# Memory rows in the order of their loads, its late pieces on SyncE between the weight chunks, and a new order for x's norms

## The chip, the cores and the metric

The kernel runs on one core of a Trainium2 chip. The metric is device time in microseconds (us) of one execution, lower is better. Before the change three runs gave 817.77, 818.16 and 818.42 us (median 818.16).

## What is computed

One encoder layer on `x` (512 rows of 1024 columns, float32) with 256 memory rows `mem`. The start, which the change touches, is this part of the reference:

```python
u = rmsnorm(h, g_mix[l])
proj = u @ w_in[l]
...
mkv = rmsnorm(mem, g_mem[l]) @ w_mem_kv[l]
mk, mv = jnp.split(mkv, 2, axis=-1)
```

After it come three branches (gated linear attention, forgetting attention, attention into the memory rows), which are gated, merged, projected and added to `x`; then an MLP with squared ReLU and a last norm. None of that is touched.

## The kernel before, in words

Every float32 operand is split in two: `hi` is the value cast to fp32r (on ScalarE), `lo` is the rest (a subtraction on VectorE). A product is three matmuls: hi by hi, hi by lo, lo by hi. TensorE's order is written out by hand; the other engines' instructions are placed by a scheduler, with `issue_after` (here `behind`) fixing the order where it matters. Weights come as chunks of 128x1024 from `wst`, in the order of `chunk_list`.

The start, in the pool "front", runs like this:

- **Warm-up.** Ten matmuls of zeros (`wz`, L288) on TensorE, which nothing waits for.
- **Loads.** SyncE issues, in this order: `cols_s` (L289: 24 columns with `g_mix`, `g_mem` and `g_gla_head`), the memory-key weight chunks 0 to 3 (L268, `raw`; chunk 0 in two halves), chunk 4 (the first of the memory-value weights), two row tiles of `x` (L314, `xn`), the identity (L331, a part of `cst_s`), chunk 5, and two more tiles of `x`. ScalarE issues the transposed memory `memr` in four pieces of two k-tiles each (L291). A k-tile is 128 of the 1024 columns of `mem`.
- **Keys.** For each k-tile, ScalarE forms `mxh` = memory times `g_mem` (L299) and VectorE `mxl` (L301); for each half chunk ScalarE casts `hi` (L272) and VectorE forms `lo` (L274). TensorE needs both: 12 matmuls of 256 columns for each k-tile (`mem_keys`, L353), 8 k-tiles.
- **Values.** 12 matmuls of 512 columns for each of the value chunks 4 and 5 (`mem_values`, L367). Chunks 6 and 7 follow between the transposes, with weights that come through L140, L147 and L148 (`raw`, `whi`, `wlo`).
- **x.** For each row tile t: sum of squares on ScalarE (L320, `xsq`, `ssx`), `ms` on VectorE (L216), its power of -1/2 on GpSimd (L217, `rr`), and the scaling in place on VectorE (L323). Then TensorE transposes `xn` against the identity (L381): k-tiles 0 and 1 first, row tiles 0 to 2 of both and then row tile 3 of both. For each k-tile `uhi` (ScalarE, L384) and `ulo` (VectorE, L385) empty the PSUM bank, and the bank is then free for a later k-tile.

From there on TensorE works through the projections (L157 to L159) and the rest of the layer.

A tile of the pool "weights" has three buffers, so chunk 5 takes the buffer of chunk 0 when that one's `lo` is done, and the weights after it follow in the same way. A transfer also carries one of eight completion counters in turn (DMAHW0 to DMAHW7 in the rows below); the ninth waits until the first has landed, and so on.

Of the kernel before, what the change touches and what calls it, by code (L numbers as in the profile page):

```python
# [9 lines left out]
F32 = mybir.dt.float32  # L10
# [51 lines left out]


@with_exitstack
def hybrid_block(ctx, tc, chunks, wst, memT, xN, cols, gffn, gfin, wup, cst, out):
    nc = tc.nc
    PSUM = bass.MemoryType.PSUM
    index = {c: i for i, c in enumerate(chunks)}
# [3 lines left out]
    def nm(s):  # L72
        uid[0] += 1
        return f"{s}_{uid[0]}"
# [28 lines left out]
    gmix, gmem, ghead = cols_s[:, 0:8], cols_s[:, 8:16], cols_s[:, 16:20]  # L103
# [109 lines left out]
    def rsqrt(pool_, ss, inv, n):  # L213
        ms = pool_.tile([P, n], F32, tag="ms", name=nm("ms"), bufs=2)
        r = pool_.tile([P, n], F32, tag="rr", name=nm("rr"), bufs=2)
        nc.vector.tensor_scalar(ms, ss, inv, EPS, op0=ALU.mult, op1=ALU.add)  # L216
        nc.gpsimd.tensor_tensor(r, ms, mhalf[:, :n], op=ALU.pow)  # L217
        return r
# [33 lines left out]

    with pool("front") as fp:
        rmb = gv[:, 0, 0:M]
        memr = fp.tile([P, KT, M], F32, name="memr")
        xn = fp.tile([P, NT, D], F32, name="xn")
        ssx = small(fp, NT, "ssx")
        pre = {}

        def lead(key, loads=1, parts=1, after=(None, None, None)):  # L260

            late = index[key] in (3, 4)
            raw = (fp if late else wp).tile([P, 1024], F32, tag="lead" if late else "raw", name=nm("raw"), bufs=2 if late else 3)
            hi, lo = pre[key] = [wp.tile([P, 1024], F32R, tag=g, name=nm(g)) for g in ("hi", "lo")]
            for i in range(loads):
                sl = slice(i * 1024 // loads, (i + 1) * 1024 // loads)
                with behind(after[0]):
                    d = nc.sync.dma_start(raw[:, sl], wst[index[key]][:, sl]).ins  # L268
            for i in range(parts):
                sl = slice(i * 1024 // parts, (i + 1) * 1024 // parts)  # L270
                with behind(after[1]):
                    a = nc.scalar.copy(hi[:, sl], raw[:, sl]).ins  # L272
                with behind(after[2]):
                    v = nc.vector.tensor_tensor(lo[:, sl], raw[:, sl], f(hi[:, sl]), op=ALU.subtract).ins  # L274
# [9 lines left out]
        warm = fp.tile([P, 1], F32, name="warm")  # L284
        nc.vector.memset(warm, 0.0)
        ps = at_()
        for _ in range(10):
            nc.tensor.matmul(ps, wz[:, :P], wz, start=True, stop=True)  # L288
        nc.sync.dma_start(cols_s, cols)  # L289
# [4 lines left out]
        vec = None  # L294
        for j in range(4):
            parts = None
            for k in (2 * j, 2 * j + 1):
                with behind(act):
                    act = nc.scalar.mul(mxh[:, k, :], memr[:, k, :], gmem[:, k:k + 1]).ins  # L299
                with behind(vec):  # L300
                    vec = nc.vector.scalar_tensor_tensor(mxl[:, k, :], memr[:, k, :], gmem[:, k:k + 1], f(mxh[:, k, :]),  # L301
                                                         op0=ALU.mult, op1=ALU.subtract).ins
                if parts is None:
                    parts = lead(chunks[j], 1 if j else 2, 2, (None, act, vec))
                    _, act, vec = next(parts)
# [4 lines left out]
        load, act, vec = next(lead(chunks[4], after=(None, act, vec)))  # L310
# [5 lines left out]
        def x_norm(t):  # L316

            sq = fp.tile([P, D], F32, tag="xsq", name=nm("xsq"), bufs=2)
            with behind(act):
                a = nc.scalar.activation(sq, xn[:, t, :], AF.Square, accum_out=ssx[:, t:t + 1]).ins  # L320
            with behind(vec):
                r = rsqrt(fp, ssx[:, t:t + 1], 1.0 / D, 1)
            return a, nc.vector.tensor_scalar(xn[:, t, :], xn[:, t, :], r, None, op0=ALU.mult).ins  # L323
# [1161 lines left out]
def layout(inputs):  # L1485
# [3 lines left out]
    x = np.asarray(inputs["x"])[0]  # L1489
    mem = np.asarray(inputs["mem"])[0]  # L1490
    chunks = chunk_list()
    wst = np.zeros((len(chunks), P, 1024), np.float32)
    for i, c in enumerate(chunks):
# [4 lines left out]
        elif c[0] == "B":  # L1498
            _, q, h, (kh, ch) = c
            j = 8 * q + 4 * h + int(kh) - 1  # L1500
# [9 lines left out]
        elif c[0] == "F":  # L1510
            _, q, h, (kh, ch) = c
            ks = slice(512 * (int(kh) - 1), 512 * int(kh))
            for n in range(2):
                j = 8 * q + 4 * h + 2 * n + int(ch) - 1
                b = W["w_ff1"][ks, j * P:(j + 1) * P].reshape(4, P, P).transpose(1, 0, 2)
# [3 lines left out]
        else:  # L1519
            g = wst[i].reshape(P, KT, P)  # L1520
# [10 lines left out]
    cols[:, 16:20] = np.asarray(inputs["g_gla_head"])[0].T  # L1531
    wup = np.zeros((P, 264), np.float32)
    wup[0:16, 0:256] = np.asarray(inputs["w_alpha_up"])[0]
    wup[16:24, 256:264] = np.eye(8, dtype=np.float32)
# [12 lines left out]
    cst[:, 4 * P:5 * P] = same & (s > t)  # L1547
    cst[:, 5 * P:] = np.where(t > s, np.float32(NEG), 0.0)
    arrays = {
        "wst": wst, "memT": tl(mem), "xN": np.ascontiguousarray(x), "cols": cols,  # L1550
        "gffn": np.ascontiguousarray(np.broadcast_to(np.asarray(inputs["g_ffn"])[0], (P, D))),
        "gfin": np.ascontiguousarray(np.broadcast_to(np.asarray(inputs["g_final"]), (P, D))),
        "wup": wup, "cst": cst,
# [24 lines left out]
```

## Time and profile before

| | |
|---|---|
| median of 3 runs | 818.16 us (817.77 to 818.42) |
| the profiled execution | 817.71 us |
| its span, first to last instruction | 815.9 us |
| TensorE busy | 805.8 us (99% of the span) |
| VectorE, ScalarE, GpSimd busy | 590.5, 438.5, 103.3 us |
| first matmul on real data starts | 6.28 us |
| first transposes of x start | 24.69 us |

In rows of the timeline the columns are start, duration, engine, line, operation, output<-inputs, count, and in brackets the idle time before it with what ended it. A row in which several instructions are merged has the time of all of them. "SPq" and "ACTq" are the issue of transfers by SyncE and ScalarE, not the transfers. A matmul's duration includes its way through the array, so two in a row overlap: what one costs in a stream is the distance from start to start.

### The profile page before, as it was taken

To read this page: it belongs to the slowest core of one execution; us is meant where nothing else is said; L and a number is where in the kernel's file an instruction comes from. 1 tells how busy PE (TensorE), PEld (TensorE's weight loads), DVE (VectorE), ACT (ScalarE), POOL (GpSimd) and SP (SyncE) were. 2 spreads that over 40 slices of the span, in tenths; PEclk is the share of its full clock that TensorE was granted. 3 is DMA by queue.
4 is the path that set the end of the run, shared out by engine and by line. 5 is a ranking of instruction groups with operands and counts; after the bars stand their busy time and mean duration, and the time that the engine had idled before them with its cause. 6 is when DMAs were issued, how large, how long until landed. Compare 5 with 4: busy or idle time off the path is not lost.

```text
span 815.9 us, 12429 instructions
## 1 busy us (share of the span) xinstructions
PE 805.8 (99%) x4789; PEld 707.8 (87%) x4789; DVE 590.5 (72%) x912; ACT 438.5 (54%) x694; POOL 103.3 (13%) x126
## 2 busy tenths in 40 slices
PE   8999999999999999999999999999999999999996
PEld 6888888888888888999999889988998899889984
DVE  5756878636465577877567648896789778887896
ACT  7745655543345234444444526774676467647764
POOL 0000110010101112134133000011001100100011
PEclk9999999999999999999999999999999999999998
DMA  9534667589689876767755604878758966896643
GB/s 337 180 104 155 181 181 202 178 235 260 189 233 278 232 232 182 164 172 187 203 152 155 206 2 160 269 161 223 236 170 190 218 213 176 192 251 200 157 81 126
DMA packets 38748, 155.53 MB, mean 191 GB/s; under 512 B 4704, under 2 KB 5152, under 8 KB 36640
## 3 DMA queue, kind: packets, MB, share of 16 engines
q1 hardware_dynamic: 27280, 95.47, 33.6%
q0 software_dynamic: 9328, 54.01, 32.0%
q10 hardware_dynamic: 2080, 5.26, 2.0%
q8 instruction: 37, 0.61, 0.3%
q14 instruction: 23, 0.19, 0.1%
HBM read 152.58 MB, written 31.49 MB: 226 GB/s over the span
## 4 chain that ended last, share of the span: by engine, by line
PE 96%; DVE 1%; DMA 1%; issue 1%; ACT 0%; SPq 0%; POOL 0%; POOLq 0%; DVEq 0%; ACTq 0%
PE mm L157 24%; PE mm L159 24%; PE mm L158 24%; PE a L158 5%; PE a L157 5%; PE a L159 5%; PE a L367 1%; PE mm L353 1%; DMA raw<-in_wst_dram 1%; PE a L597 1%; PE a L635 1%; PE a L634 1%; DVE h L1240 1%; PE a L873 1%; DVE lo L1246 0%
## 5 line engine op out<-in xcount | busy, mean ns | idle before, releaser
L148 DVE TENSOR_TENSOR wlo<-raw,whi 128x1024 fp32r<-128x1024 f32 x67 | 86.6, 1297 | 58.9 <-ACT whi L147 58.5
L157 PE MATMUL mm<-uhi,whi 128*128 128x512 f32 (+1 forms) x352 | 125.9, 358 | 0.0
L159 PE MATMUL mm<-uhi,wlo 128*128 128x512 f32 (+1 forms) x352 | 123.7, 351 | 0.0
L158 PE MATMUL mm<-ulo,whi 128*128 128x512 f32 (+1 forms) x352 | 123.6, 351 | 0.0
L147 ACT CAST whi<-raw 128x1024 fp32r<-128x1024 f32 x67 | 70.5, 1052 | 91.5 <-PE mm L158 55.0
L1244 ACT CAST hi<-raw 128x1024 fp32r<-128x1024 f32 x65 | 68.2, 1049 | 49.6 <-PE mm L158 34.4
L1246 DVE TENSOR_TENSOR lo<-raw,hi 128x1024 fp32r<-128x1024 f32 x65 | 79.5, 1222 | 17.4 <-ACT hi L1244 17.4
L157 PEld LDWEIGHTS mm<-uhi,whi 128*128 128x128 f32 x352 | 66.7, 189 | 9.9 <-issue 1.4
L159 PEld LDWEIGHTS mm<-uhi,wlo 128*128 128x128 f32 x352 | 66.6, 189 | 9.1
L158 PEld LDWEIGHTS mm<-ulo,whi 128*128 128x128 f32 x352 | 66.7, 189 | 8.1
L1244 ACT CAST hi<-b 128x1024 fp32r<-128x1024 f32 x40 | 41.9, 1048 | 42.0 <-PE mm L159 25.5
L158 PE MATMUL mm<-u2l,hi 128*128 128x256 f32 x224 | 63.4, 283 | 0.0
L159 PE MATMUL mm<-u2h,lo 128*128 128x256 f32 x224 | 63.4, 283 | 0.0
L157 PE MATMUL mm<-u2h,hi 128*128 128x256 f32 x224 | 63.4, 283 | 0.0
L1430 POOL DMA_DIRECT2D b<-in_wst_dram x32 | 27.3, 853 | 271.3 <-DVE lo L1246 206.7
L1246 DVE TENSOR_TENSOR lo<-b,hi 128x1024 fp32r<-128x1024 f32 x40 | 48.8, 1222 | 14.1 <-ACT hi L1244 14.0
L157 PE MATMUL mm<-hi,ch 128*128 128x512 f32 x136 | 52.9, 389 | 0.0
L158 PE MATMUL mm<-lo,ch 128*128 128x512 f32 x136 | 52.9, 389 | 0.0
L159 PE MATMUL mm<-hi,cl 128*128 128x512 f32 x136 | 52.9, 389 | 0.0
L157 PE MATMUL mm<-u2sh,hi 128*128 128x256 f32 x168 | 47.6, 283 | 0.0
L158 PE MATMUL mm<-u2sl,hi 128*128 128x256 f32 x168 | 47.6, 283 | 0.0
L159 PE MATMUL mm<-u2sh,lo 128*128 128x256 f32 x168 | 47.6, 283 | 0.0
(412 smaller groups left out, 2091.8 us busy)
## 6 DMA issues: line engine op xcount, KB each, us to landing
raw<-in_wst_dram SPq DMA_DIRECT2D x114, 512.0 KB
b<-in_wst_dram POOLq DMA_DIRECT2D x32, 512.0 KB, 5.5
raw<-T SPq DMA_DIRECT2D x28, 512.0 KB
T<-in_wst_dram POOLq DMA_DIRECT2D x12, 1024.0 KB, 8.9
b<-in_wst_dram SPq DMA_DIRECT2D x16, 512.0 KB
wb<-in_wst_dram POOLq DMA_DIRECT2D x15, 512.0 KB, 5.4
wb<-in_wst_dram SPq DMA_DIRECT2D x8, 512.0 KB
nFb<-dF ACTq DMA_DIRECT2D x6, 512.0 KB
```

Source lines behind the costliest of these rows:

```text
L147: cast = nc.scalar.copy(hi, raw)
L148: low_now[0] = nc.vector.tensor_tensor(lo, raw, f(hi), op=ALU.subtract).ins
L157: nc.tensor.matmul(ps, lh, rh, start=start, stop=False, skip_group_check=on)
L158: nc.tensor.matmul(ps, lh, rl, start=False, stop=False, skip_group_check=on)
L159: nc.tensor.matmul(ps, ll, rh, start=False, stop=stop, skip_group_check=on)
L353: nc.tensor.matmul(kps[h], w[:, h * P:(h + 1) * P], x[:, k, :], start=k == p == 0, stop=k == KT - 1 and p == 2)
L367: nc.tensor.matmul(ps, x[:, k, sl], w[low][:, kk, :], start=k == low == 0 and x is mxh, stop=k == KT - 1 and low == 1)
L597: nc.tensor.matmul(ps[e], q[a, sl], k[a, :w], start=p == 0, stop=p == 2)
L634: nc.tensor.matmul(po[:, q0:], vv, PTh[:, c0:c0 + w], start=n == 0, stop=False)
L1244: nc.scalar.copy(hi, raw)
L1246: nc.vector.tensor_tensor(lo, raw, f(hi), op=ALU.subtract)
L1430: nc.gpsimd.dma_start(to[i], wst[index["B", q, i, x]], accum_op=ALU.add)
```

## The change

1. `cols_s` is no longer loaded by itself. Its 24 columns stand in DRAM behind the rows of the first memory piece, and land with them in one tile `mem_s` of 2072 columns; `g_mem` is read from there, and GpSimd copies the 24 columns to `cols_s` for the later uses.
2. Memory in DRAM: each of the four pieces is a block of its own, in the order of the loads (before: each piece was 2 KB out of rows of 8 KB). In SBUF the k-tiles stand in reverse order, so that the first piece is next to the 24 columns.
3. ScalarE issues pieces 0 and 1. SyncE issues piece 2 between weight chunks 1 and 2, and piece 3 between chunks 2 and 3.
4. Nine warm-up matmuls, not ten.
5. Norms of x: chunk 5's load and split come before the scaling of row tile 1; row tiles 1 and 2 are scaled one after the other; row tile 3 is scaled in two parts (256 and 768 columns). The identity is loaded behind the last row tile of x.

```diff
-        for _ in range(10):
+        for _ in range(9):
             nc.tensor.matmul(ps, wz[:, :P], wz, start=True, stop=True)
-        nc.sync.dma_start(cols_s, cols)
-        for j in range(4):
-            d = nc.scalar.dma_start(memr[:, 2 * j:2 * j + 2], memT[:, 2 * j:2 * j + 2]).ins
+        def mem_load(eng, j, end=0, after=None):
+            n = 2 * M
+            at = j and j * P * n + P * 24
+            with behind(after):
+                return eng.dma_start(mem_s[:, (3 - j) * n:(4 - j) * n + end],
+                                     memT[at:at + P * (n + end)].rearrange("(p c) -> p c", p=P)).ins
+
+        mem_load(nc.scalar, 0, 24)
+        d = mem_load(nc.scalar, 1)
...
         for j in range(4):
             parts = None
+            if j > 1:
+                load = mem_load(nc.sync, j, after=load)
...
+        nc.gpsimd.tensor_copy(cols_s, mem_s[:, KT * M:])
...
-        for t in range(NT):
-            if t == 2:
-                load, act, vec = next(lead(chunks[5], after=(load, act, vec)))
-            load = x_load(t)
-            act, vec = x_norm(t)
+        for t in range(2):
+            load = x_load(t)
+            act, vec, r = x_square(t)
+            if t == 0:
+                vec = x_scale(t, r)
+        load, act, vec = next(lead(chunks[5], after=(load, act, vec)))
+        load = x_load(2)
+        act, vec, r2 = x_square(2)
+        vec = x_scale(1, r)
+        vec = x_scale(2, r2)
+        load = x_load(3)
+        act, vec, r = x_square(3)
+        x_scale(3, r, (0, 2 * P, D))
         x_act = act
-        nc.sync.dma_start(ident, cst[:, :P])
+        with behind(load):
+            nc.sync.dma_start(ident, cst[:, :P])
```

`x_square` holds the square (ScalarE), `ms` (VectorE) and the power (GpSimd) of one row tile, `x_scale` its scaling.

SyncE's transfers from its first one on, before (`raw_160` is chunk 0 in two halves, `raw_173` to `raw_209` chunks 1 to 4, `raw_231` chunk 5; "waits" names what must have landed or been done before the issue):

```order
L289 DMA cols_s<-in_cols_dram 128x24
L268 DMA raw_160<-in_wst_dram 128x512 x2
L268 DMA raw_173<-in_wst_dram 128x1024
L268 DMA raw_185<-in_wst_dram 128x1024 [waits DMAHW0_49]
L268 DMA raw_197<-in_wst_dram 128x1024 [waits DMAHW1_49]
L268 DMA raw_209<-in_wst_dram 128x1024 [waits DMAHW2_49]
L314 DMA xn<-in_xN_dram 128x1024 [waits DMAHW3_49]
L314 DMA xn<-in_xN_dram 128x1024 [waits DMAHW4_49]
L331 DMA cst_s<-in_cst_dram 128x128 [waits DMAHW5_49]
L268 DMA raw_231<-in_wst_dram 128x1024 [waits DMAHW6_49,DVE_49]
```

And now (`raw_156` is chunk 0, `raw_169` to `raw_208` chunks 1 to 4, `raw_229` chunk 5):

```order
L270 DMA raw_156<-in_wst_dram 128x512 x2
L270 DMA raw_169<-in_wst_dram 128x1024
L295 DMA mem_s<-in_memT_dram 128x512
L270 DMA raw_182<-in_wst_dram 128x1024
L295 DMA mem_s<-in_memT_dram 128x512
L270 DMA raw_195<-in_wst_dram 128x1024 [waits DMAHW0_49]
L270 DMA raw_208<-in_wst_dram 128x1024 [waits DMAHW1_49]
L325 DMA xn<-in_xN_dram 128x1024 [waits DMAHW2_49]
L325 DMA xn<-in_xN_dram 128x1024 [waits DMAHW3_49]
L270 DMA raw_229<-in_wst_dram 128x1024 [waits DMAHW4_49,DVE_49]
L325 DMA xn<-in_xN_dram 128x1024 [waits DMAHW5_49]
L325 DMA xn<-in_xN_dram 128x1024 [waits DMAHW6_49]
```

The first weights move to the front of the queue, two memory pieces stand between the weights, and the identity, which stood ahead of chunk 5, now follows the last row here (which row tile 3 of x is).

VectorE from the `lo` of chunk 4 to the first `ulo`, before:

```order
L274 TENSOR_TENSOR lo_211<-raw_209,hi_210 128x1024
L216 TENSOR_SCALAR ms_218<-ssx_134 128x1
L323 TENSOR_SCALAR xn<-xn,rr_219 128x1024
L216 TENSOR_SCALAR ms_226<-ssx_134 128x1
L323 TENSOR_SCALAR xn<-xn,rr_227 128x1024
L274 TENSOR_TENSOR lo_233<-raw_231,hi_232 128x1024
L216 TENSOR_SCALAR ms_240<-ssx_134 128x1
L323 TENSOR_SCALAR xn<-xn,rr_241 128x1024
L216 TENSOR_SCALAR ms_248<-ssx_134 128x1
L323 TENSOR_SCALAR xn<-xn,rr_249 128x1024
L148 TENSOR_TENSOR wlo_401<-raw_398,whi_400 128x1024
L385 SCALAR_TENSOR_TENSOR ulo<-a_384,cols_s,uhi 128x512
```

And now:

```order
L276 TENSOR_TENSOR lo_210<-raw_208,hi_209 128x1024
L333 TENSOR_SCALAR ms_217<-ssx_134 128x1
L340 TENSOR_SCALAR xn<-xn,rr_218 128x1024
L333 TENSOR_SCALAR ms_225<-ssx_134 128x1
L276 TENSOR_TENSOR lo_231<-raw_229,hi_230 128x1024
L333 TENSOR_SCALAR ms_238<-ssx_134 128x1
L340 TENSOR_SCALAR xn<-xn,rr_226 128x1024
L340 TENSOR_SCALAR xn<-xn,rr_239 128x1024
L333 TENSOR_SCALAR ms_247<-ssx_134 128x1
L340 TENSOR_SCALAR xn<-xn,rr_248 128x256
L340 TENSOR_SCALAR xn<-xn,rr_248 128x768
L148 TENSOR_TENSOR wlo_401<-raw_398,whi_400 128x1024
```

The `lo` of chunk 5 moved ahead of the scaling of row tile 1, and the last scaling became two instructions.

More of the change, by code (lines that the diff above doesn't have):

```diff
@@ L64, in hybrid_block @@
 @with_exitstack
-def hybrid_block(ctx, tc, chunks, wst, memT, xN, cols, gffn, gfin, wup, cst, out):
+def hybrid_block(ctx, tc, chunks, wst, memT, xN, gffn, gfin, wup, cst, out):
     nc = tc.nc
@@ L254, in hybrid_block @@
         rmb = gv[:, 0, 0:M]
-        memr = fp.tile([P, KT, M], F32, name="memr")
+        mem_s = fp.tile([P, KT * M + 24], F32, name="mem_s")
+        memr = mem_s[:, :KT * M].rearrange("p (k m) -> p k m", k=KT)
+        gmem = mem_s[:, KT * M + 8:KT * M + 16]
         xn = fp.tile([P, NT, D], F32, name="xn")
@@ L309, in hybrid_block @@
         nc.gpsimd.memset(mhalf, -0.5)
-        load, act, vec = next(lead(chunks[4], after=(None, act, vec)))
+        nc.gpsimd.tensor_copy(cols_s, mem_s[:, KT * M:])
+        load, act, vec = next(lead(chunks[4], after=(load, act, vec)))
         def x_load(t):
@@ L320, in x_norm, with x_scale @@
                 a = nc.scalar.activation(sq, xn[:, t, :], AF.Square, accum_out=ssx[:, t:t + 1]).ins
+            ms, r = (fp.tile([P, 1], F32, tag=g, name=nm(g), bufs=2) for g in ("ms", "rr"))
             with behind(vec):
[L322 to L329 removed]
+                m = nc.vector.tensor_scalar(ms, ssx[:, t:t + 1], 1.0 / D, EPS, op0=ALU.mult, op1=ALU.add).ins
+            nc.gpsimd.tensor_tensor(r, ms, mhalf[:, :1], op=ALU.pow)
+            return a, m, r
+        def x_scale(t, r, cols=(0, D)):
+            for sl in (slice(a, b) for a, b in zip(cols, cols[1:])):
+                with behind(vec):
+                    v = nc.vector.tensor_scalar(xn[:, t, sl], xn[:, t, sl], r, None, op0=ALU.mult).ins
+            return v
+        for t in range(2):
+            load = x_load(t)
+            act, vec, r = x_square(t)
[9 more added lines that the diff above has]
+        x_scale(3, r, (0, 2 * P, D))
         x_act = act
[L331 removed]
+        with behind(load):
+            nc.sync.dma_start(ident, cst[:, :P])
         get_plain = get_w
@@ L1531, in layout @@
     cols[:, 16:20] = np.asarray(inputs["g_gla_head"])[0].T
+    pairs = [tl(mem)[:, 2 * j:2 * j + 2][:, ::-1].reshape(P, -1) for j in range(4)]
+    mem_flat = np.concatenate([np.concatenate([pairs[0], cols], axis=1).ravel()] + [x.ravel() for x in pairs[1:]])
     wup = np.zeros((P, 264), np.float32)
```

16 lines of the change are left out of this document (8 added, 8 removed).

## Prediction

> **What bounds the kernel.** I start with the page: the busy time of the engines, and the chain that ended last.
>
> ```profile
> PE 805.8 (99%) x4789; PEld 707.8 (87%) x4789; DVE 590.5 (72%) x912; ACT 438.5 (54%) x694; POOL 103.3 (13%) x126
> PE 96%; DVE 1%; DMA 1%; issue 1%; ACT 0%; SPq 0%; POOL 0%; POOLq 0%; DVEq 0%; ACTq 0%
> ```
>
> TensorE is the bound, so time can only be won where it stands still. The view of waits, for TensorE over the whole span, has two rows:
>
> ```profile
> PE mm L353 <- ACT hi L272: 1.5, 3, 0.6
> PE a L288 <- DVE warm L285: 1.2, 1, 1.2
> ```
>
> The second is the start before the warm-up. The first, three waits, lies in the key products, where the change works. The timeline of those microseconds:
>
> ```profile
> 0.74 0.38 SPq L289 DMA_DIRECT2D cols_s<-in_cols_dram  x1
> ...
> 1.18 5.31 SPq L268 DMA_DIRECT2D raw<-in_wst_dram  x6
> 1.19 4.45 PE L288 MATMUL a<-wz 128*128 128x512 bf16 x10 [1.19 <-DVE warm L285]
> ...
> 4.55 0.51 ACT L299 ACTIVATE mxh<-memr,cols_s 128x256 fp32r<-128x256 f32 x1 [0.42 <-DMA memr<-in_memT_dram]
> ...
> 5.61 0.62 ACT L272 CAST hi<-raw 128x512 fp32r<-128x512 f32 x1 [0.56 <-DMA raw<-in_wst_dram]
> ...
> 6.28 0.74 PE L353 MATMUL mm<-mxh,hi 128*128 128x256 f32 x4 [0.64 <-ACT hi L272]
> ...
> 6.86 0.64 PE L353 MATMUL mm<-mxl,hi 128*128 128x256 f32 x4
> ...
> 7.83 0.62 ACT L272 CAST hi<-raw 128x512 fp32r<-128x512 f32 x1 [1.19 <-DMA raw<-in_wst_dram]
> ...
> 8.50 0.74 PE L353 MATMUL mm<-mxh,hi 128*128 128x256 f32 x4 [0.53 <-ACT hi L272]
> ...
> 9.81 0.62 ACT L272 CAST hi<-raw 128x512 fp32r<-128x512 f32 x1 [0.96 <-DMA raw<-in_wst_dram]
> ...
> 10.49 0.74 PE L353 MATMUL mm<-mxh,hi 128*128 128x256 f32 x4 [0.29 <-ACT hi L272]
> ```
>
> Three times TensorE waits for a cast, and the cast for a transfer: the halves of chunk 0 land at 5.6 and 7.8, chunk 1 at 9.8. The chain in order of time shows the same and what follows:
>
> ```profile
> 2.12 7.68 DMA raw<-in_wst_dram
> 9.79 0.02 issue
> 9.81 0.63 ACT hi L272
> 10.44 0.04 issue
> 10.49 8.89 PE mm L353 x72
> 19.38 5.47 PE a L367 x24
> ```
>
> From 10.49 on TensorE has no hole until the transposes. The 72 matmuls of six k-tiles take 8.89, **1.48 a k-tile**. All eight would need 11.85, yet 6.28 to 19.38 is 13.10: **1.25 us are lost after the first matmul**, and more before it. Are the transfers limited by bytes? The windows, whose last columns are DMA share and GB/s:
>
> ```profile
> 2.25:4.50 2.25, 2.25 (x6) 0.75 (x5) 0.00 (x0) 1.49 (x2) 0.00 (x0) 1.00 0.95 215
> 4.50:6.75 2.25, 1.61 (x7) 0.62 (x6) 0.97 (x2) 1.53 (x3) 0.00 (x0) 1.00 1.03 346
> 6.75:9.00 2.25, 1.72 (x15) 1.52 (x14) 1.12 (x3) 1.03 (x2) 0.00 (x0) 1.00 1.03 401
> ```
>
> Yes: the engines are full, at 346 to 401 GB/s after a slow beginning. What is asked for first then arrives first, and the order of the bytes is worth time.
>
> **Part 1: memory pieces and columns.** Before chunk 1 was there, the queues had carried the columns (12 KB), four memory pieces (1049 KB; all issued early by ScalarE, taking turns with the weights) and chunks 0 and 1 (1049 KB). Now pieces 2 and 3 stand behind chunk 1, 524 KB less ahead of it. At 401 GB/s that is 1.3 us: chunk 1 at 8.5. The second half of chunk 0 loses one piece of 262 KB ahead of it, 0.7 us: 7.1. The first half had shared with most of piece 1, 262 KB at 346: 0.75, so 4.9. The removed issue of the columns also lets SyncE's first weights go out at 0.74, not 1.18. That is worth 0 to 0.44; these landings count none of it.
>
> The first `mxh` waited for piece 0 and the columns until 4.55. Now they are one transfer of 274 KB, and I leave its landing at 4.5. So: `mxh` 0.51 to 5.05, cast 0.62 to 5.7, first matmul at **5.7** (6.28 before; nine warm-up matmuls end 0.44 earlier, at 5.2, and are not in the way). Its k-tile ends at 7.2. The second half at 7.1, cast and 0.05 on: 7.8 (8.50 before), done at 9.3. Chunk 1 at 8.5, cast until 9.15: there in time. So chunk 1's matmuls start at **9.3, against 10.49: 1.2 us**, and with the 0.44 of the earlier queue in full at 8.85: 1.65. I take **1.4**, about the middle.
>
> Behind it nothing may be late. Piece 2 and chunk 2 are 786 KB, 2.0 us behind chunk 1: 10.5, cast by 11.1, and TensorE wants them at 12.1 (9.1 and two k-tiles). Piece 3 and chunk 3 come 2.0 later again, cast by 13.1, and are wanted at 15.0. After them the bytes asked for are those of before. The copy of the columns on GpSimd costs nothing: GpSimd idles until 17.5 in this row, and the columns are wanted at the first `uhi`, 25.65. No row shows this copy; between nothing and the 0.55 of a one-column power, I take 0.2, all hidden. Reversed k-tiles cost nothing: the same elements are read.
>
> ```profile
> 17.50 0.55 POOL L217 TENSOR_TENSOR rr<-ms,mhalf 128x1 f32<-128x1 f32 x1 [16.52 <-DVE ms L216]
> ```
>
> **Part 2: x.** If TensorE comes 1.4 earlier, is x ready? The timeline there:
>
> ```profile
> 20.24 1.22 DVE L274 TENSOR_TENSOR lo<-raw,hi 128x1024 fp32r<-128x1024 f32 x1
> ...
> 21.35 1.06 ACT L320 ACTIVATE xsq<-xn 128x1024 f32<-128x1024 f32 x1 [1.06 <-DMA xn<-in_xN_dram]
> ...
> 22.92 0.15 DVE L216 TENSOR_SCALAR ms<-ssx 128x1 f32<-128x1 f32 x1
> ...
> 23.21 0.55 POOL L217 TENSOR_TENSOR rr<-ms,mhalf 128x1 f32<-128x1 f32 x1 [0.99 <-DVE ms L216]
> ...
> 23.79 0.75 DVE L323 TENSOR_SCALAR xn<-xn,rr 128x1024 f32<-128x1024 f32 x1 [0.73 <-POOL rr L217]
> 24.46 1.22 DVE L148 TENSOR_TENSOR wlo<-raw,whi 128x1024 fp32r<-128x1024 f32 x1
> 24.69 1.03 PE L381 MATMUL a<-cst_s,xn 128*128 128x128 f32 x8
> ...
> 26.38 1.41 DVE L385 SCALAR_TENSOR_TENSOR ulo<-a,cols_s,uhi 128x512 fp32r<-128x512 f32 x2 [0.70 <-ACT uhi L384]
> ...
> 28.03 1.27 ACT L384 ACTIVATE uhi<-a,cols_s 128x512 fp32r<-128x512 f32 x2 [1.11 <-PE a L381]
> ...
> 28.75 1.41 DVE L385 SCALAR_TENSOR_TENSOR ulo<-a,cols_s,uhi 128x512 fp32r<-128x512 f32 x2 [0.97 <-ACT uhi L384]
> ...
> 29.56 1.31 PE L381 MATMUL a<-cst_s,xn 128*128 128x128 f32 x8
> ```
>
> Row tile 3 of x lands last, at 21.3. In the old order TensorE would gain about 0.8 at most: `xn` 3 is done at 24.54, and its transposes come six (0.6) behind 24.69. In the new one the identity (64 KB, 0.16 us at 401 GB/s) no longer stands ahead, and the queue may start up to 0.44 earlier: it lands at 21.0 (20.7 to 21.3). Square and its read 1.15 until 22.2; `ms` then finds VectorE free, since the `lo` of chunk 5 (20.24) now goes ahead of the waiting scaling and the backlog is gone: 22.3. Power and scaling follow at the old distances: 23.2. The first 256 columns cost 0.2 (a bound of 0.15 is the one-column `ms`, 0.75 the whole), and TensorE's transposes of them start at 23.4; at 1.4 earlier they are due at 23.9, so the split holds. The other 768 columns end at 24.0, `wlo` at 25.2, the first pair of `ulo` at 26.6 (27.8 before, 1.2 earlier), and the fourth k-tile's transposes, which need the bank that the second `ulo` empties, end at 27.0. `uhi`, `ulo` and the next transposes follow from the third k-tile, turned from 25.9 (the first `ulo` of the pair) for 0.5, half of the 1.03 of eight; with 0.1 to `uhi`, and the distances 0.72 and 0.81 between the starts of the last three rows, 28.0 instead of 29.56. This way **allows 1.4 to 1.5**, and 1.2 with the landing unchanged at 21.3. The split adds an instruction to VectorE, about 0.1 us, counted in it.
>
> **Sum.** The smaller of 1.4 (keys) and 1.45 (x), less 0.05 for seams: **1.35 us** off. What comes later finds TensorE without a wait to the end, so it is kept whole. From the profiled execution's own 817.71 it makes 816.36. That execution lies 0.45 under the median of the runs shown, so for a median I give **816.8**.
>
> **A rule of the Trainium skill against it.** The Trainium skill, "DMA: Bandwidth & Descriptors", section "Issuing engines are not separate DMA queues", says that transfers issued by different engines run on the same DMA engines and mix, and that spreading issues saves only the issuing time. The windows agree (401 GB/s with both queues at work). By it, the change of issuer in itself would be worth no more than the 0.44 of issue; the rest would have to come from the order of bytes, which is how the sum is made.
>
> **Rivals.**
>
> (B) *More is won: 1.9 us, 815.8 from the profile, 816.25 as a median.* The strided memory pieces cost more for a byte than the weights. Up to 20 us:
>
> ```profile
> q1 hardware_dynamic: 1953, 5.65, 71.7%
> q10 hardware_dynamic: 576, 1.05, 19.7%
> ```
>
> ScalarE's queue (q10, memory) took 19.7% for 1.05 MB, 0.188 a MB; SyncE's 0.127. As a block, two pieces at the lower price save 0.524 times 0.061 times 20 = 0.6 us ahead of chunk 1. Then the first matmul starts near 5.3, chunk 1 at 8.3 and TensorE gains 2.2; x, landing at 20.7 or before, allows 1.7 to 2. Against it: the queue that starts first pays for the slow beginning, whatever it carries.
>
> (C) *Less is won: 0.5, 817.65.* The early transfers are limited by the beginning (215 GB/s until 4.5) and by the slowest engine, not by bytes. Then chunk 1 lands at 9.3, and x no earlier. For it: that window. Against: 401 GB/s from 6.75 on.
>
> (D) *Slower: 0.7, 818.9.* TensorE runs slowly at first. The ten warm-up matmuls are 0.44 apart for 512 columns (4.45 for ten); later ones are 0.23 apart:
>
> ```profile
> 19.22 0.40 PE L367 MATMUL a<-hi,mxh 128*128 128x512 f32 x1
> 19.45 0.40 PE L367 MATMUL a<-hi,mxl 128*128 128x512 f32 x1
> ```
>
> The first group of real ones (0.58 from 6.28 to the next at 6.86, against 0.49, a third of 1.48) is still partly slow. If the warm-up with nine matmuls is too short, or real work arrives before the speed does, the slow time goes on, at worst as long again as the 4.45 of the warm-up, from 5.7 until 10.8: in 5.1 us 2.6 of work are done out of the 2.9 of the first two k-tiles, and chunk 1 starts at 11.2, 0.7 later than before. It decides when speed comes after about 8; until 6.4, as before, the wait for the second half (7.2 to 7.8) covers it. The Trainium skill, "TensorE: Matmul & The Clock Gate", section "Part 1: The HAM clock gate (the "warmup" mystery)", gives the window of activity as 3.4 us and free-running, so that by it the moment would differ between executions of one kernel; the trace agrees on two speeds with a ratio near two, and one profile can't show the rest.
>
> **How the numbers follow.** Forecast 0.55 (0.9 to 1.64 off; 816.5 to 817.3 as a median), B 0.28, C 0.10, D 0.07. About 0.2% (1.64 us) is what a measurement can tell from no change: B lies beyond it, with a few hundredths of the forecast's upper end; of D only a tail (two such slow times, or an unseen stall) reaches it. Faster 0.32, same 0.63, slower 0.05. The range goes from B's end to between C and D: 815.9 to 818.2.
>
> **What would show it.** Right: the first L353 matmul near 5.7, chunk 1's near 9.2, no more than two short waits of TensorE for the casts (L274), `xsq` of row tile 3 near 21.0, the L408 transposes of x from about 23.3, the fifth k-tile's near 28.0. B: first matmul by 5.3. C: chunk 1's cast after 9.3. D: matmuls of 256 columns 0.21 apart after 6.5. Wrong altogether: a new wait of TensorE behind 30 us, or x's transposes waiting for `ident` or `cols_s`.

## The result and the profile after

The changed kernel takes 816.24 us (median of 12 runs, 815.97 to 816.66), the kernel before beside it 817.84 (12 runs, 817.45 to 818.65). The ratio is 0.998, its 95% interval 0.9971 to 0.9989: about 1.6 us less (0.9 to 2.4). The profiled execution takes 815.97 us with a span of 814.2, 1.74 less than the one of before. In later series some runs of the changed kernel take about 2 us more than the rest, near 818.3; the third group of experiments is about them, and where it matters I give the two groups of runs apart.

The page of the changed kernel, the busy times and the chain that ended last:

```profile
PE 805.0 (99%) x4788; PEld 707.4 (87%) x4788; DVE 590.2 (72%) x913; ACT 438.7 (54%) x694; POOL 103.9 (13%) x127
...
PE 96%; DVE 1%; issue 1%; DMA 0%; ACT 0%; POOL 0%; POOLq 0%; DVEq 0%; ACTq 0%
```

TensorE is as much the bound as it was. Of the 1.7 us by which the span is shorter, 0.9 were idle time of TensorE (815.9 less 805.8 before, 814.2 less 805.0 now) and 0.8 busy time, 0.58 of it the warm-up, which nothing waits for (4.45 before, 3.87 now). Its waits over the whole span:

```profile
PE a L290 <- DVE warm L287: 1.2, 1, 1.2
PE mm L380 <- ACT hi L274: 0.5, 1, 0.5
```

Three waits for casts (1.5 us) became one of 0.5, and no new one came. The timeline of the first microseconds, where the key products are now L380, the casts L274, `mxh` L309 and the copy of the columns L320:

```profile
1.19 3.87 PE L290 MATMUL a<-wz 128*128 128x512 bf16 x9 [1.19 <-DVE warm L287]
...
4.46 0.51 ACT L309 ACTIVATE mxh<-mem_s 128x256 fp32r<-128x256 f32 x1 [1.30 <-DMA mem_s<-in_memT_dram]
...
4.50 0.20 POOL L320 COPY cols_s<-mem_s 128x24 f32<-128x24 f32 x1 [3.52 <-DMA mem_s<-in_memT_dram]
...
4.88 0.60 ACT L274 CAST hi<-raw 128x512 fp32r<-128x512 f32 x1
...
5.53 0.74 PE L380 MATMUL mm<-mxh,hi 128*128 128x256 f32 x4 [0.47 <-ACT hi L274]
...
5.80 0.60 ACT L274 CAST hi<-raw 128x512 fp32r<-128x512 f32 x1
...
7.07 0.64 PE L380 MATMUL mm<-mxh,hi 128*128 128x256 f32 x4
...
7.09 0.62 ACT L274 CAST hi<-raw 128x512 fp32r<-128x512 f32 x1 [0.27 <-DMA raw<-in_wst_dram]
...
8.51 0.64 PE L380 MATMUL mm<-mxh,hi 128*128 128x256 f32 x4
```

Read the brackets. The first two casts (4.88 and 5.80) wait for no transfer any more; the third, chunk 1's at 7.09, waits 0.27, but TensorE wants its result only at 8.51. The cast takes 0.62 and TensorE starts about 0.05 behind it, so the result would be ready for TensorE at 7.76: chunk 1 lands at 7.1, 0.75 us earlier than it must, and TensorE runs from its first real matmul on without a hole. Chunk 1's products start at 8.51 instead of 10.49: **1.98 us**, of which 0.75 is the earlier first matmul (5.53, not 6.28) and 1.23 the holes behind it. The chain in order of time has lost its stop at a cast of chunk 1:

```profile
0.74 3.70 DMA mem_s<-in_memT_dram
4.44 0.02 issue
4.46 0.51 ACT mxh L309
4.97 0.52 ACT hi L274
5.49 0.04 issue
5.53 11.78 PE mm L380 x96
17.31 5.61 PE a L394 x24
```

The start now hangs on the first memory piece alone. The windows of the transfers (the last column is GB/s):

```profile
2.25:4.50 2.25, 2.25 (x6) 0.76 (x5) 0.00 (x0) 0.94 (x3) 0.00 (x1) 1.00 0.91 333
4.50:6.75 2.25, 1.77 (x12) 1.22 (x11) 1.72 (x4) 2.25 (x5) 0.20 (x1) 1.00 1.03 408
6.75:9.00 2.25, 2.25 (x22) 2.25 (x21) 2.11 (x5) 1.98 (x5) 0.00 (x0) 1.00 1.06 418
```

They were 215, 346 and 401. The slow beginning, which my sum left as it was, is much less slow. Then x (the row at 21.20 is the scaling of row tile 2):

```profile
20.05 1.07 ACT L330 ACTIVATE xsq<-xn 128x1024 f32<-128x1024 f32 x1 [0.15 <-DMA xn<-in_xN_dram]
...
21.20 0.75 DVE L340 TENSOR_SCALAR xn<-xn,rr 128x1024 f32<-128x1024 f32 x1 [0.44 <-POOL rr L334]
...
21.87 0.15 DVE L333 TENSOR_SCALAR ms<-ssx 128x1 f32<-128x1 f32 x1
...
22.16 0.55 POOL L334 TENSOR_TENSOR rr<-ms,mhalf 128x1 f32<-128x1 f32 x1 [0.99 <-DVE ms L333]
...
22.75 0.89 DVE L340 TENSOR_SCALAR xn<-xn,rr 128x256 f32<-128x256 f32 x2 [0.73 <-POOL rr L334]
22.76 1.03 PE L408 MATMUL a<-cst_s,xn 128*128 128x128 f32 x8
...
27.70 1.32 PE L408 MATMUL a<-cst_s,xn 128*128 128x128 f32 x8
```

Row tile 3 of x is there at 20.0, not 21.3. The transposes start at 22.76 (24.69 before: 1.93 earlier), those of the fifth k-tile at 27.70 (29.56: 1.86). The first L157 matmul starts 1.82 earlier, the last matmul of the program 1.80 (806.41 against 808.21). The gain of the start is carried to the end nearly whole.

### The profile page after: what moved, and what is told of

It is laid out like the page before. It is cut to its first block, busy times and chain, and to the rows that moved or that the text cites. A ratio compares the mean times of both kernels' runs of the same rounds, so it can differ in the third digit from the quotient of the medians.

```text
span 814.2 us, 12430 instructions
## 1 busy us (share of the span) xinstructions
PE 805.0 (99%) x4788; PEld 707.4 (87%) x4788; DVE 590.2 (72%) x913; ACT 438.7 (54%) x694; POOL 103.9 (13%) x127
## 4 chain that ended last, share of the span: by engine, by line
PE 96%; DVE 1%; issue 1%; DMA 0%; ACT 0%; POOL 0%; POOLq 0%; DVEq 0%; ACTq 0%
PE mm L157 24%; PE mm L158 24%; PE mm L159 24%; PE a L157 5%; PE a L158 5%; PE a L159 5%; PE mm L380 1%; PE a L394 1%; PE a L624 1%; PE a L662 1%; PE a L661 1%; DVE h L1267 1%; PE a L900 1%; PE a L408 1%; DMA mem_s<-in_memT_dram 0%
## 5 line engine op out<-in xcount | busy, mean ns | idle before, releaser
L157 PE MATMUL mm<-uhi,whi 128*128 128x512 f32 (+1 forms) x352 | 125.9, 358 | 0.0
L157 PEld LDWEIGHTS mm<-uhi,whi 128*128 128x128 f32 x352 | 66.7, 189 | 9.9 <-issue 1.5
L157 PE MATMUL mm<-u2h,hi 128*128 128x256 f32 x224 | 63.4, 283 | 0.0
L157 PE MATMUL mm<-hi,ch 128*128 128x512 f32 x136 | 52.9, 389 | 0.0
L157 PE MATMUL mm<-u2sh,hi 128*128 128x256 f32 x168 | 47.5, 283 | 0.0
```

The source lines that it names most:

```text
L157: nc.tensor.matmul(ps, lh, rh, start=start, stop=False, skip_group_check=on)
```

## The experiments

My theory after the result: TensorE gains what the holes and the late first matmul cost, and the parts of the change overlap, because each of them alone makes chunk 0 or 1 earlier. The rivals are that one part does it all, and for x that the new order of its norms is needed for the last microsecond.

### One part undone

Each of these four is the changed kernel with one part as it was before; the kernel before has a median of 818.1 beside them (33 runs).

**a1_old_x**: the norms of x and the identity in the order of before.

```diff
-        for t in range(2):
-            load = x_load(t)
-            act, vec, r = x_square(t)
...
+        for t in range(NT):
+            if t == 2:
+                load, act, vec = next(lead(chunks[5], after=(load, act, vec)))
+            load = x_load(t)
+            act, vec = x_norm(t)
         x_act = act
-        with behind(load):
-            nc.sync.dma_start(ident, cst[:, :P])
+        nc.sync.dma_start(ident, cst[:, :P])
```

> The changed kernel with x's norms and the identity's load in the old order; loads of memory, columns and weights as changed. Theory X (the working on record: the old order allows about 0.8 us of gain before row tile 3 is late): the keys are as after the change (value products start at 17.15), but the transposes of row tile 3 or the ulo behind them wait, and 0.8 to 1.0 us of the 1.6 are lost: 817.0 to 817.2. Rival: row tile 3 itself landed about a microsecond earlier after the change (its square starts at 20.05, not 21.35), so the old order is in time too: less than 0.3 us lost.

Measured: 816.62 (11 runs), ratio 0.9988 (0.9979 to 0.9996). Six runs lie at 815.95 to 816.62 (median 816.24), five at 817.95 to 818.46. Its timeline (the transposes are L392 here):

```profile
20.44 1.06 ACT L331 ACTIVATE xsq<-xn 128x1024 f32<-128x1024 f32 x1
...
22.82 1.20 PE L392 MATMUL a<-cst_s,xn 128*128 128x128 f32 x8
```

The last square follows the one of row tile 2 without a wait: row tile 3 of x is there by 20.4 in the old order too, although the identity stands ahead of it. The transposes start 0.06 later than in the changed kernel, the first L157 matmul 0.13 later (36.34 against 36.21). So **the new order of the norms is worth about 0.1 us here**. The rival's reading holds. x came earlier with the old order too, because everything in the queues moved up: added over the windows, a1 had carried 3.58 MB by 11.25 us, the kernel before 3.17 MB, and the 0.4 MB between them are about 1.0 us at 415 GB/s (the rate of a1's last window).

**a2_rows**: the four pieces lie in DRAM as strips of long rows again.

```diff
-            at = j and j * P * n + P * 24
...
-                                     memT[at:at + P * (n + end)].rearrange("(p c) -> p c", p=P)).ins
+                                     memT[:, (3 - j) * n:(4 - j) * n + end]).ins
...
-    mem_flat = np.concatenate([np.concatenate([pairs[0], cols], axis=1).ravel()] + [x.ravel() for x in pairs[1:]])
+    mem_flat = np.ascontiguousarray(np.concatenate(pairs[::-1] + [cols], axis=1))
```

> The changed kernel, only that memory and columns lie in DRAM as rows of 8.3 KB of which each piece takes 2 KB, as before, and not as blocks; every issue as changed. Theory BLOCKS (rival B of the prediction: strided pieces cost more for a byte): pieces 0 and 1 take about 0.6 us longer, chunk 1's matmuls (third k-tile) start near 9.1 instead of 8.51, the time is 0.4 to 0.6 us longer. Theory ORDER (only the bytes ahead count): no change within 0.15 us, third k-tile near 8.5.

Measured: 816.54 (11 runs), ratio 0.9985 (0.9977 to 0.9994); eight runs at 816.25 to 817.09 (median 816.53), three near 818.2. The window of its beginning:

```profile
2.25:4.50 2.25, 2.25 (x6) 0.76 (x5) 0.00 (x0) 0.91 (x2) 0.00 (x0) 1.00 0.92 269
```

269 GB/s instead of 333, the first `mxh` at 5.04 instead of 4.46. In this profile, of an execution near 818.2, the first matmul starts at 6.10 instead of 5.53, and chunk 1's cast (7.66) is still ahead of its use. So the rows cost the start about half a microsecond by this one profile, as theory BLOCKS had it; by the lower groups of the runs it is 0.1 to 0.3 (816.53 against 816.43 and 816.24 for the changed kernel).

**a3_scalar4**: all four pieces issued by ScalarE.

```diff
-        d = mem_load(nc.scalar, 1)
+        for j in range(1, 4):
+            d = mem_load(nc.scalar, j)
...
-            if j > 1:
-                load = mem_load(nc.sync, j, after=load)
```

> The changed kernel, only that all four memory pieces are issued by ScalarE at the start; blocks, columns and x as changed. Theory ORDER: 524 KB are again ahead of chunk 1, which lands 1.3 us later than the 7.06 to 7.1 after the change: the second half of chunk 0 near 6.3, chunk 1 near 8.4, the third k-tile's matmuls near 9.1 instead of 8.51, 0.5 to 0.7 us lost. Theory BLOCKS: the order is worth little, third k-tile by 8.7, at most 0.2 us lost.

Measured: 816.42 (11 runs), ratio 0.9985 (0.9976 to 0.9994); eight runs at 816.19 to 816.54 (median 816.33), three at 817.8 to 818.2. Chunk 1's cast starts at 7.83, 0.74 later than in the changed kernel, its products at 8.77, without a hole. The landing moved as theory ORDER said, by 0.74 instead of 1.3, and the time did not, as theory BLOCKS said.

**a4_columns**: the columns as a transfer of their own, first in SyncE's queue.

```diff
+        nc.sync.dma_start(cols_s, cols)
-        mem_load(nc.scalar, 0, 24)
+        mem_load(nc.scalar, 0)
...
-        nc.gpsimd.tensor_copy(cols_s, mem_s[:, KT * M:])
```

> The changed kernel, only that the columns are again a transfer of their own, first on SyncE, so that the weights are issued 0.44 us later; memory blocks, order of pieces and x as changed, no copy on GpSimd. Theory FRONT: the first mxh waits for the columns or the first cast for the later weights, the first matmul starts near 6.0 instead of 5.53, and 0.3 to 0.5 us are lost to the end. Rival: the beginning is limited by the engines' start and not by the issue; first matmul by 5.7, at most 0.15 us lost.

Measured: 816.56 (11 runs), ratio 0.9981 (0.9973 to 0.999); nine runs at 816.12 to 816.79 (median 816.43), two near 818.1. The first piece is even earlier (`mxh` at 3.70), but now the first cast waits for its weights:

```profile
5.05 0.62 ACT L274 CAST hi<-raw 128x512 fp32r<-128x512 f32 x1 [0.84 <-DMA raw<-in_wst_dram]
```

The first matmul starts at 5.72, chunk 1's cast at 7.78. The times agree with the rival.

What follows from the four: **no single part is needed.** Chunk 1's cast starts at 7.22 (a1), 7.66, 7.83 and 7.78, by at most 0.74 later than 7.09, just within the 0.75 that it has to spare. The changed kernel itself, in a later series, has 816.43 as the median of its lower seven runs (the run of the third group); none of the four is outside that by more than the runs scatter, so a part worth less than about 0.3 us would not show. Times of one profile scatter too: in the five profiles with the loads of the changed kernel (its own and the four of the third group) the first `mxh` starts between 4.46 and 4.77, chunk 1's cast between 7.09 and 7.38.

### One part alone on the kernel before

The other side of the same question; the kernel before has 818.2 beside these (27 runs).

**b2_blocks**: only the layout in DRAM, each piece a block.

```diff
-            d = nc.scalar.dma_start(memr[:, 2 * j:2 * j + 2], memT[:, 2 * j:2 * j + 2]).ins
+            d = nc.scalar.dma_start(memr[:, 2 * j:2 * j + 2], memT[j]).ins
...
-        "memT": tl(mem),
+        "memT": np.stack([tl(mem)[:, 2 * j:2 * j + 2] for j in range(4)]),
```

> The kernel before, only that each memory piece is a block of its own in DRAM. Undoing single parts of the change left nearly all of the gain, though each made chunk 1 land later (7.1 us after the change; 7.7 with rows, 7.8 with four pieces on ScalarE, 7.8 with the columns by themselves; 9.8 before). Theory SUM: the parts add up in the landing, and TensorE needs chunk 1 only by about 8, so that each alone takes chunk 1 to about 9.1 and its matmuls to about 9.8 (10.49 before): 0.6 us faster, 817.5. Rival (one cause): blocks alone bring nearly all, 816.6 or less.

Measured: 817.15 (11 runs), ratio 0.9987 (0.9978 to 0.9995), about 1.0 us less. Two rows of its timeline, then the window of its beginning:

```profile
6.30 0.74 PE L353 MATMUL mm<-mxh,hi 128*128 128x256 f32 x4 [1.15 <-ACT hi L272]
...
9.58 0.74 PE L353 MATMUL mm<-mxh,hi 128*128 128x256 f32 x4 [0.16 <-ACT hi L272]
```

```profile
2.25:4.50 2.25, 2.25 (x6) 0.76 (x5) 0.00 (x0) 1.86 (x3) 0.00 (x0) 1.00 0.96 302
```

The first matmul is no earlier, but the hole ahead of the second k-tile is gone, and chunk 1's products start 0.91 earlier. That is near theory SUM (9.58; it had 9.8).

**b3_order**: only pieces 2 and 3 moved to SyncE, behind chunks 1 and 2.

```diff
-        for j in range(4):
-            d = nc.scalar.dma_start(memr[:, 2 * j:2 * j + 2], memT[:, 2 * j:2 * j + 2]).ins
+        for j in range(2):
+            d = mem_load(nc.scalar, j)
...
+            if j > 1:
+                load = mem_load(nc.sync, j, after=load)
```

> The kernel before, only that SyncE issues memory pieces 2 and 3, behind chunks 1 and 2 (rows in DRAM, the columns by themselves first, old order of x). Theory SUM: chunk 1 lands near 9.0, its matmuls start near 9.7, the first matmul stays near 6.3; 0.7 us faster, 817.4. Rival (the order alone is the gain, as the working on record had it): first holes gone, 816.6 or less.

Measured: 817.11 (11 runs), ratio 0.9987 (0.9978 to 0.9996), about 1.1 us less. Its first products:

```profile
7.00 0.74 PE L359 MATMUL mm<-mxh,hi 128*128 128x256 f32 x4 [1.72 <-ACT hi L272]
...
9.97 0.64 PE L359 MATMUL mm<-mxh,hi 128*128 128x256 f32 x4
```

The first matmul is 0.72 *later* than before (the first half of chunk 0 is cast at 6.33, not 5.61), and still TensorE gains half a microsecond by chunk 1 (9.97 against 10.49), since both holes behind it are gone. What counts is when the last hole ends, not when the first matmul starts. Three of its runs lie at 818.5 to 818.9, the other eight at 816.7 to 817.3; the next group bears on that, for it has a hole of 1.72 behind its warm-up.

**b5_columns**: only the columns with the first piece; rows, four pieces on ScalarE, ten warm-up matmuls and x as before. Relative to the changed kernel it is the edits of a1, a2 and a3 together, and

```diff
-        for _ in range(9):
+        for _ in range(10):
```

> The kernel before, only that the columns come with the first memory piece (rows in DRAM, four pieces on ScalarE, ten warm-up matmuls, old order of x; k-tiles reversed in SBUF). Theory SUM: the first matmul near 5.8, chunk 1 near 9.1 and its matmuls near 9.8; 0.6 us faster, 817.5. Rival: the 0.44 us of the earlier issue is all, the first matmul moves by 0.4 and the holes behind it grow by as much: 818.0.

Measured: 816.58 (9 runs, 816.27 to 816.87), ratio 0.9977 (0.9967 to 0.9986), **about 1.6 us less**. Neither my sum nor its rival had that. Two rows:

```profile
8.23 0.62 ACT L274 CAST hi<-raw 128x512 fp32r<-128x512 f32 x1 [0.86 <-DMA raw<-in_wst_dram]
...
9.07 0.64 PE L362 MATMUL mm<-mxh,hi 128*128 128x256 f32 x4
```

Chunk 1 lands at 8.2, not 9.8, by this part alone, and its products start at 9.07 without a hole. SyncE's queue (q1) shows why it can: packets, MB and share of what it had moved between 1.5 and 2.8 us, before and in b5:

```profile
q1 hardware_dynamic: 134, 0.01, 9.0%
```

```profile
q1 hardware_dynamic: 52, 0.11, 36.2%
```

The 0.01 MB are the columns. With them as a transfer of their own at the head of the queue, the first packet of weights starts at 3.07 (2.84, 2.98 and 2.87 in b2, b3 and a4), and without it at 1.75 to 1.78 in all the other kernels: 1.1 to 1.3 us earlier, though the issue is only 0.44 earlier. The next window, from 4.50 to 6.75, shows the same division: 346, 397, 338 and 330 GB/s (before, b2, b3, a4) against 408 to 421 in the others, b5 with 418 among them.

Alone the three bring 1.0, 1.1 and 1.6 (by the medians; the intervals of the ratios are 0.4 to 1.8, 0.3 to 1.8 and 1.1 to 2.7), together 1.6: they fill the same holes. Once chunk 1 is there before it is wanted, the next part has only the start of the first matmul to win.

### The number of warm-up matmuls

The runs near 818.3 were in all four kernels of the first group, each with nine warm-up matmuls. The theory: in those runs TensorE's speed comes late, because the warm-up ends before real work is there. The rival: these runs have nothing to do with the warm-up. One number is changed (`for _ in range(9):` to 6, 10 and 11), with the changed kernel again as **a0_after**; the kernel before has 818.19 (32 runs).

```diff
-        for _ in range(9):
+        for _ in range(10):
```

> The changed kernel once more, beside the next three on one chip. In the four runs before this one the times of each kernel fall into two groups, about 816.3 and 818.2, and the one profile from the upper group (the row layout) has matmuls of 256 columns 0.21 us apart until 9.6 us, not 0.12. Theory SPEED (rival D of the prediction): TensorE's speed-up comes at its own moment and needs the warm-up to reach up to real work; the hole of 0.5 us between the ninth warm-up matmul and 5.53 sometimes loses it, for this kernel too: a part of the runs near 818.2. Rival: the two groups belong to the changes of those four kernels; all runs at 816.0 to 816.7.

> The changed kernel with six warm-up matmuls instead of nine; the hole before real work grows from 0.5 to 1.7 us. Theory SPEED: most runs fall into the slow group, near 818.2 or up to 819, and the profile shows matmuls 0.21 apart until 9 to 10 us. Rival (the number of warm-up matmuls does not matter): 816.0 to 816.7.

> The changed kernel with ten warm-up matmuls as before; the tenth ends at about 5.5, where real work starts, so there is no hole. Theory SPEED: no run near 818.2, all at 816.0 to 816.7, nothing lost at the start (first real matmul 5.55 to 5.65). Rival (the groups have another cause, such as the transfers): the same share of slow runs as with nine.

> The changed kernel with eleven warm-up matmuls, which end near 5.95 and hold up real work by 0.4 us. Theory SPEED: no slow runs; 0.1 to 0.4 us longer than with ten in the fast group, since the second half of chunk 0 and chunk 1 are there already and the delay is not made up. Rival: the same share of slow runs as with nine.

| warm-up matmuls | median (runs) | ratio | runs over 817.6 |
|---|---|---|---|
| 6 | 817.83 (11) | 0.9994 (0.9985 to 1.0002) | 8 of 11 |
| 9 (the changed kernel) | 816.74 (11) | 0.9985 (0.9976 to 0.9995) | 4 of 11 |
| 10 | 816.26 (11) | 0.9979 (0.997 to 0.9988) | 0 of 11 |
| 11 | 816.36 (11) | 0.998 (0.9971 to 0.9989) | 0 of 11 |

The profiled execution of a0_after is one of the four, with 818.43:

```profile
1.20 4.02 PE L290 MATMUL a<-wz 128*128 128x512 bf16 x9 [1.20 <-DVE warm L287]
...
5.79 1.22 PE L380 MATMUL mm<-mxh,hi 128*128 128x256 f32 x4 [0.57 <-ACT hi L274]
...
6.80 1.05 PE L380 MATMUL mm<-mxl,hi 128*128 128x256 f32 x4
...
9.36 1.05 PE L380 MATMUL mm<-mxl,hi 128*128 128x256 f32 x4
10.22 0.81 PE L380 MATMUL mm<-mxh,lo 128*128 128x256 f32 x4
10.86 0.64 PE L380 MATMUL mm<-mxh,hi 128*128 128x256 f32 x4
```

Compare the distances from start to start: 0.85 for four matmuls (0.21 each) until 10.2, 0.64 for the four in which the speed changes (at about 10.6), then 0.48 (0.12 each). All nine warm-up matmuls ran at the slow speed (4.02 for nine), ended at 5.22, and after a hole of 0.57 TensorE went on slowly for more than four microseconds. Chunk 1's products start at 10.86 instead of 8.51, and the first L157 matmul at 38.56 instead of 36.21: 2.35 later, about what those runs are longer. The profile's column of the granted clock says 1.00 all the while; only the distances show it. With ten matmuls:

```profile
1.19 3.62 PE L290 MATMUL a<-wz 128*128 128x512 bf16 x10 [1.19 <-DVE warm L287]
5.74 0.74 PE L380 MATMUL mm<-mxh,hi 128*128 128x256 f32 x4 [0.93 <-ACT hi L274]
```

Here the ten took only 3.62, so the speed had come during the warm-up, and the hole of 0.93 behind it did no harm. Ten matmuls at 0.43 would have lasted until 5.64, to the edge of the real work. The profile of c6_warm is of one of its three executions under 817.6 (816.49), so the matmuls 0.21 apart that were expected in it are not there:

```profile
1.20 2.74 PE L290 MATMUL a<-wz 128*128 128x512 bf16 x6 [1.20 <-DVE warm L287]
5.64 0.74 PE L380 MATMUL mm<-mxh,hi 128*128 128x256 f32 x4 [1.71 <-ACT hi L274]
6.22 0.64 PE L380 MATMUL mm<-mxl,hi 128*128 128x256 f32 x4
```

All six warm-up matmuls were 0.43 apart, the hole is 1.71, and yet the real work runs at full speed from 5.64. The same is seen in a4 (nine at 0.43, a hole of 0.51). So a hole ahead of the speed makes the loss possible, not certain; what decides in one execution is not shown. The theory holds by the counts: 4 of 11 and 8 of 11 against 0 of 22 on one chip. The tenth matmul costs nothing (816.26), and in this series **the changed kernel with ten warm-up matmuls is ahead of both kernels**: the mean of its eleven runs is 816.35, that of the eleven with nine beside them 817.15. Its lead over nine lies in the runs near 818.3 alone.

### The first piece in two transfers

With the holes gone, the start hangs on piece 0 (`mxh` at 4.46). **d1_split** loads the columns and the first k-tile by themselves.

```diff
-        mem_load(nc.scalar, 0, 24)
+        c0 = (KT - 1) * M
+        nc.scalar.dma_start(mem_s[:, c0:], memT[:P * (M + 24)].rearrange("(p c) -> p c", p=P))
+        nc.scalar.dma_start(mem_s[:, c0 - M:c0], memT[P * (M + 24):P * (2 * M + 24)].rearrange("(p c) -> p c", p=P))
```

> The changed kernel with memory piece 0 in two transfers: k-tile 0 with the columns (1.1 KB rows), then k-tile 1. Theory FIRST: the first mxh then starts near 4.1 instead of 4.5, the first matmul near 5.2, right behind the nine warm-up matmuls, so that there is hardly a hole: 0.3 us faster than the changed kernel in its fast group (815.9) and hardly a slow run. Rival: the landing is limited by the beginning and not by the size of the piece: first matmul at 5.5 or later, 816.2 and the same slow runs.

Measured: 816.32 (7 runs, one of them 818.2), ratio 0.9978 (0.9966 to 0.9989), which is what the changed kernel has. The profile:

```profile
5.45 1.21 PE L382 MATMUL mm<-mxh,hi 128*128 128x256 f32 x4 [0.24 <-ACT hi L274]
...
6.47 0.67 PE L382 MATMUL mm<-mxl,hi 128*128 128x256 f32 x4
```

Half the bytes land only 0.08 earlier (`mxh` at 4.38), less than profiles of one kernel differ by, and the first four matmuls fall into the slow time of this execution (1.02 from start to start). The third `mxh`, which needs memory piece 1, now waits for it until 7.32 (6.31 and no wait before the split). The first matmul at 5.45 lies between theory and rival, and the time is the rival's: the split wins nothing.

## Why the prediction was right in direction and short in size

The forecast was 1.35 us off, 816.8; measured were 1.6 off and 816.24, and 1.74 between the two profiled executions. The absolute times hold some luck: the kernel before has 817.84 beside the changed one, not the 818.16 that I subtracted from. From 817.84 the forecast's 1.35 gives 816.49 and B's 1.9 gives 815.94, and 816.24 lies halfway. Point by point:

- **The bound and the holes: right.** The late first matmul and TensorE's waits for the casts are where the time came from, and of the 1.98 us at chunk 1's products 1.80 are left at the last matmul.
- **The mis-sized term is Part 1's landings**: "At 401 GB/s that is 1.3 us: chunk 1 at 8.5", and the second half of chunk 0 at 7.1. Chunk 1 came at 7.1, the second half by 5.8, and the keys gained 1.98, not 1.4. I had taken the beginning (215 GB/s until 4.5) as given and only moved bytes behind it. The 1.4 us that were missed for chunk 1 can be booked from the windows: 118 GB/s more from 2.25 to 4.50 are 266 KB, 0.66 us at 401; 62 GB/s more from 4.50 to 6.75 are 140 KB, 0.35; and by its landing (both windows until 2.25 show 30 GB/s or less) the queues had carried 1.87 MB, of which 1.59 had to be there, 0.29 being for later use. Before, at 9.79, it was about 2.55 of 2.11, 0.44 for later use: 0.15 MB less now, 0.37. Together 1.38.
- **What sped up the beginning** was rival B's reason, and the runs bear it out: with blocks the window from 2.25 to 4.50 shows 333, 325, 319 and 347 GB/s (changed kernel, a1, a3, a4) and 302 (b2, blocks alone); with rows 215 (before), 269 (a2), 220 (b3) and 238 (b5). My objection ("the queue that starts first pays for the slow beginning, whatever it carries") was wrong. B's time, 816.25, was nearly hit as well, by the luck above. But B's way from there to the time does not hold as it stands: with rows (a2) the kernel is hardly slower, for chunk 1 still comes before it is wanted. And b5 shows 1.6 without any block.
- **The other half of the beginning is the head of SyncE's queue.** I put "0 to 0.44" on the removed issue of the columns and counted none of it in the landings. The first packet of weights starts at 1.76 now and at 3.07 before: 1.3 earlier. In b5, which changes this and keeps the rows, chunk 1 lands 1.58 earlier, and the same booking gives 0.22 MB more carried by 6.75 us (0.55 at 401) and 0.04 MB for later use at its landing instead of 0.44 (1.0).
- **The first matmul**: 5.53, between my 5.7 and B's 5.3.
- **x**: row tile 3 at 20.0 (I said 21.0, at best 20.7). "In the old order TensorE would gain about 0.8 at most" was wrong for that reason: it rested on a landing at 21.3 that stayed, and a1 shows the old order keeping all but 0.1. The rest of that path came out in time: no wait of TensorE for x, 1.93 earlier at the transposes, and VectorE's split scaling hidden. One step in it was wrong: `ms` does not find VectorE free. It starts at 21.87, behind the scaling of row tile 2 (21.20, 0.75), so the landing, 1.0 earlier than I had it, brings the scaling of row tile 3 only from 23.2 to 22.75.
- **The warm-up with nine "not in the way"**: true in the profile after, not in every run. Rival D's mechanism is real: in the runs concerned the products after the hole run slowly until about 10, chunk 1's products start at 10.86 (a0_after; D had 11.2), and the time is near 818.3. Between the profiled executions (818.43 and 817.71) that is D's 0.7 above the kernel before; against that kernel's median (818.19) it is 0.1. One sign that I read for D was none: 0.58 for the first four real matmuls is not a rest of the slow time, for every group behind a hole begins so, at 8.50 (the next at 9.08) and at 10.49 (11.06) too. In the first series no run lay there (0 of 12), later 4 of 11, so the 816.24 is also lucky: the median of a0_after is 816.74.
- **The copy of the columns on GpSimd**, put at 0.2 and hidden, took 0.20 and is hidden.
- **Issuers**: the Trainium skill, "DMA: Bandwidth & Descriptors", section "Issuing engines are not separate DMA queues", gives the choice of issuer in itself no more than the time of issuing. No run here tests that alone: a3 changes issuer and order together, which makes chunk 1 0.74 later and no measurable time.

Open stays why the weights' first packet comes 1.3 us earlier when the issue is only 0.44 earlier: b5 drops a transfer of 128 short rows at the head of SyncE's queue and issues the weights earlier, and no run parts the two. a4, which brings the short transfer back beside blocks, has the late start (2.87) and yet no measurable loss. Open is also why the first twelve runs had none near 818.3.

## What to carry to other kernels

When several edits fill the same hole, each looks good alone and none is missed when it is taken away: find the slack behind the landing (here 0.75 us, with the cast that follows it taken off) before crediting a part. In a sum of transfers, do not keep the beginning's rate fixed when the layout of the first transfers changes, or what stands at the head of a queue. And let the warm-up of TensorE reach the first real matmul: an extra matmul that nobody waits for costs nothing, one too few costs 2 us in some of the runs.

## What was unexpected of the hardware

- The speed of TensorE comes at different moments in executions of one kernel: within the warm-up (3.62 for ten matmuls in c10_warm), at about 6.5 (d1_split) or at about 10.6 (a0_after). The Trainium skill, "TensorE: Matmul & The Clock Gate", section "Part 1: The HAM clock gate (the "warmup" mystery)", has a window of activity of 3.4 us that runs freely. That the moment differs agrees; the spread of more than six microseconds is wider than one such window. By the same section a clock that has been granted is lost after an idle window of about 3.4 us. Here a hole of 0.57, ahead of the speed, went with a delay of more than four microseconds (a0_after), and the counts by the number of warm-up matmuls say that such holes matter; holes of 0.51 (a4) and 1.71 (c6_warm) went without.
- Blocks instead of 2 KB strips of 8 KB rows raised what the DMA engines moved in their first microseconds from 215 to 302 GB/s (b2 against before), with the engines about equally busy (0.96 against 0.95).
- A transfer of 12 KB in 128 rows at the head of SyncE's queue goes with a late start of the big ones behind it: their first packet starts at 2.84 to 3.07 us in the four kernels that have it, at 1.75 to 1.78 in the ten that don't.
